# A two-layer decoder trunk on one core: the first layer's split weights kept in device memory, and the stick-breaking scans chained through a column of their own

## The chip, the core and the metric

The kernel runs on one core of one Trainium2 chip. The core has five engines with a queue of instructions each: TensorE (PE in the profile; its weight loads are listed apart as PEld), VectorE (DVE), ScalarE (ACT), GpSimd (POOL) and SyncE (SP), which here issues every DMA. The engines run side by side and wait for one another through semaphores. Data lies in device memory, in SBUF (128 partitions) and in PSUM, where matmuls accumulate.

The metric is the device time of one execution in microseconds, lower is better; each kernel is timed in several runs, and one further execution is recorded by the hardware profiler.

## The reference

The input is 2048 tokens of width 1024, with 16 learned meta tokens put in front: 2064 tokens. Two layers follow, each as h = h + post_norm(mixer(pre_norm(h))). The mixer of layer 0 has two branches from one input projection (22 blocks of 128 columns): sliding-window attention with sinks, and a convolution module. The mixer of layer 1 is stick-breaking attention, 16 heads of width 64.

```python
def swa_conv_mixer(h, pos, w_in, sinks, conv_w, conv_b, ln_g, ln_b, w_pw2, w_out):
    q, k, v, g_a, glu_in, g_b = _split(h @ w_in, AB_SPLITS)
    ...
    a = sliding_window_sink_attention(q, k, v, sinks).reshape(b, l, SWA_WIDTH) * jax.nn.silu(g_a)
    u = glu_in[..., :CONV_CHANNELS] * jax.nn.sigmoid(glu_in[..., CONV_CHANNELS:])
    c = jax.nn.silu(layer_norm(causal_depthwise_conv(u, conv_w, conv_b), ln_g, ln_b))
    c = (c @ w_pw2) * jax.nn.silu(g_b)
    return jnp.concatenate([a, c], axis=-1) @ w_out

def stick_breaking_attention(q, k, v):
    ...
        log_beta = jax.nn.log_sigmoid(z)
        log_1m = jnp.where(valid, jax.nn.log_sigmoid(-z), 0.0)
        after = lax.cumsum(log_1m, axis=3, reverse=True) - log_1m
        a = jnp.where(valid, jnp.exp(log_beta + after), 0.0)
        outs.append(jnp.einsum('bhqk,bkhd->bqhd', a.astype(v.dtype), vp[:, :kend]))
```

In words, for each query the weight of a key is sigmoid(z) times the product of sigmoid(-z) over all later valid keys. The convolution has 31 taps.

## The kernel before

**Split matmuls.** A float32 matmul is made of three in the faster format fp32r: each operand is split into a rounded half and the rest (`wh` and `wl` for weights, `hTh` and `hTl` for activations), and `mm3` (lines 126 to 130) adds high x high, high x low and low x high. A weight block is 128 x 8 x 128 floats, 512 KB. A projection of 512 tokens by one block is 24 matmuls of 512 columns.

**Layer 0.** The tokens go in four chunks (528, then three times 512). `stage1(c)` normalizes and transposes a chunk and runs the 22 projections; `stage2(c)` is the attention (`swa`) and the end of the convolution branch (`cbranch`) of the chunk. `stage1(c + 1)` is interleaved with `stage2(c)`. The weights stay in no buffer from one chunk to the next: `weights` (lines 112 to 121) is called by every projection, 22 times per chunk, and twice by each of the eight `pw` steps of `cbranch` (the two halves of `w_pw2`), 104 times in all. Each call loads the raw block into `raw` (line 118; two buffers, for `w_pw2` one that is shared with the tile `yl`), ScalarE casts it to `wh` (line 119), and GpSimd subtracts to get `wl` (line 120). `wh` and `wl` have two buffers each in the pool `pww`. The load has a priority 60 steps ahead of its place.

The 31 convolution taps are VectorE instructions (line 294), four blocks of channels per chunk; they are put into a list and recorded six at a time behind the projections. Gates, rotary products, the splits of activations and the score masks are VectorE's too; GpSimd has part of the rotary work (lines 339 to 343) and small normalization steps (lines 88 to 93). All results of stage 1 go to device memory (`q0d`, `k0d`, `v0d`, `gad`, `gbd`, `yd`) on SyncE's queue and come back in stage 2. After the last chunk comes the output projection of layer 0, interleaved with the first loads of layer 1.

**Layer 1.** The projections (`proj`, their splits in lines 109 and 110) of one pair of heads are interleaved with the attention (`attn`) of an earlier pair. `attn` takes two query blocks of 128 (`x`) and two heads (`h`) at a time and walks the keys in chunks of up to 512 from the last to the first. For each of the four (h, x) of a chunk: two matmuls give `z` (line 898); ScalarE makes `om` = sigmoid(-z/8) and `be` = sigmoid(z/8) (lines 902, 903); in the first chunk, which holds the diagonal, GpSimd masks both (line 906); VectorE scans the running product of `om` from right to left into `S` (line 910) and multiplies `be` by `S` shifted by one column (line 913). The weights are transposed (line 930), copied by ScalarE (line 936) and multiplied with the values (line 944).

The scan's start value lies in `S[:, n]`. For a first chunk GpSimd fills it with 1.0 (line 907); for the others it copies it from the tile `carry` (line 909), into which it copied the last product `S[:, 0]` of the chunk before (line 912). `om` and `S` have three buffers, `be` two for each (h, x). GpSimd also copies the weights of the meta tokens (line 915).

**The order.** The program is recorded step by step; a scheduler then orders each engine's queue by a simulated timeline and priorities. Every queue runs in order: an instruction that waits holds up all behind it. On SyncE a DMA also waits for the one eight places ahead that used the same semaphore.

Of the kernel before, what the change touches and what calls it, by code (L numbers as in the profile page):

```python
# [10 lines left out]
F32 = mybir.dt.float32  # L11
F32R = mybir.dt.float32r
I32 = mybir.dt.int32
AF = mybir.ActivationFunctionType
ALU = mybir.AluOpType
# [3 lines left out]
P = 128  # L19
D = 1024  # L20
KB = D // P
# [16 lines left out]
WP = 60  # L38
# [40 lines left out]
class Trunk:  # L79
# [29 lines left out]
        self.nc.gpsimd.tensor_scalar(hi, src, 1.0, 0.0, ALU.mult, ALU.add)  # L109
        self.nc.vector.tensor_tensor(lo, src, hi, ALU.subtract)  # L110

    def weights(self, pool, src, rpool, tag):
        nc = self.nc
        raw = rpool.tile([P, KB, P], F32, tag=tag, name="raw", bufs=2 if tag == "raw" else 1)
        wh = pool.tile([P, KB, P], F32R, tag="wh", name="wh")
        wl = pool.tile([P, KB, P], F32R, tag="wl", name="wl")
        with self.tc.high_priority(offset=WP):
            self.wdma = nc.sync.dma_start(raw, src).ins
        nc.scalar.copy(wh, raw)  # L119
        nc.gpsimd.tensor_tensor(wl, raw, wh, ALU.subtract)  # L120
        return wh, wl

    def mv(self, out, src):
# [54 lines left out]
    def layer0(self, after=None):  # L178
        tc, nc, a = self.tc, self.nc, self.a
        HALO = CW - 1  # L180
        qd = self.dram("q0d", [P, 2, 4, T], F32R)
        kd = self.dram("k0d", [2, 2, HD, T], F32R)
# [68 lines left out]
        def stage1(c):  # L251
# [23 lines left out]
            steps.append((0.0, start))  # L275

            def proj(m, evac):
                wh, wl = self.weights(pww, a["w_in0"][m], s1, "raw")
                turns = late[:]
                late.clear()  # L280
                for s0, sn in subs:
                    ps = self.bank(next(banks), "pj")
                    for k in range(KB):
                        self.mm3(ps[:, :sn], wh[:, k], wl[:, k], st["h"][:, k, s0 : s0 + sn], st["l"][:, k, s0 : s0 + sn], k == 0, k == KB - 1)
                    evac(ps[:, :sn], s0, sn)
                for f in turns:
                    f()
# [191 lines left out]
        def cbranch(ut):  # L479
            b0 = tok0(ut[0])  # L480
            N = sum(toks(t) for t in ut)
            S = {}

            def stats():
                yl = w2.tile([P, 4, 272], F32, tag="yl", name="yl", bufs=1)
                nc.sync.dma_start(yl[:, :, :N], yd[:, :, b0 : b0 + N].rearrange("r p t -> p r t"))
                mv = w2.tile([P, 3, 2], F32, tag="mv", name="mv")
                nc.vector.memset(mv, 1.0)
                S["yns"] = yns = []
                for i, t in enumerate(ut):  # L490
                    n, o = toks(t), tok0(t) - b0
                    pt = self.bank("pt", "pt_y")
                    for j in range(4):
                        nc.tensor.transpose(pt[:n, j * P : j * P + P], yl[:, j, o : o + n], self.ident)
                    st = w2.tile([P, 6], F32, tag="bst", name="bst")
                    nc.vector.bn_stats(st[:n], pt[:n])
                    nc.vector.bn_aggr(mv[:n, i], st[:n])
                    yn = w3.tile([P, 512], F32, tag="yn", name="yn")
                    nc.scalar.copy(yn[:n], pt[:n])
                    yns.append(yn)  # L500
                cr = w2.tile([P, 3], F32, tag="cr", name="cr")
                self.rsqrt(w2, cr, mv[:, :, 1], 1.0, LEPS, 3, nc.gpsimd)
                for i, t in enumerate(ut):
                    n = toks(t)
                    nc.vector.tensor_scalar(yns[i][:n], yns[i][:n], mv[:n, i, 0:1], cr[:n, i : i + 1], ALU.subtract, ALU.mult)

            def act():
                yns = S["yns"]
                S["ch"] = ch = w2.tile([P, 4, 272], F32R, tag="ch", name="ch", bufs=1)
                S["cl"] = cl = w2.tile([P, 4, 272], F32R, tag="cl", name="cl", bufs=1)  # L510
                for j in range(4):
                    pt = self.bank("pt", "pt_c")
                    for i, t in enumerate(ut):
                        n, o = toks(t), tok0(t) - b0
                        nc.tensor.transpose(pt[:, o : o + n], yns[i][:n, j * P : j * P + P], self.ident[:n, :n])
                    sg = w2.tile([P, 272], F32, tag="csg", name="csg")
                    tt = w2.tile([P, 272], F32, tag="ctt", name="ctt")
                    nc.scalar.activation(sg[:, :N], pt[:, :N], AF.Sigmoid, bias=cv[:, 2, j : j + 1], scale=cv[:, 1, j : j + 1])
                    nc.scalar.activation(tt[:, :N], pt[:, :N], AF.Identity, bias=cv[:, 2, j : j + 1], scale=cv[:, 1, j : j + 1])
                    nc.vector.tensor_tensor(tt[:, :N], tt[:, :N], sg[:, :N], ALU.mult)  # L520
                    nc.scalar.copy(ch[:, j, :N], tt[:, :N])
                    nc.vector.tensor_tensor(cl[:, j, :N], tt[:, :N], ch[:, j, :N], ALU.subtract)

            def pw():
                ch, cl = S["ch"], S["cl"]
                gb = w2.tile([P, 4, 272], F32, tag="gb", name="gb", bufs=1)
                nc.sync.dma_start(gb[:, :, :N], gbd[:, :, b0 : b0 + N].rearrange("r p t -> p r t"))
                for m in range(4):
                    if m % 2 == 0:
                        wh, wl = self.weights(pww, a["w_pw2"][m // 2], w2, "yl")  # L530
                    ps = self.bank("pj", "pw")
                    for k in range(4):
                        kk = 4 * (m % 2) + k
                        self.mm3(ps[:, :N], wh[:, kk], wl[:, kk], ch[:, k, :N], cl[:, k, :N], k == 0, k == 3)
                    tt = w2.tile([P, 272], F32, tag="ctt", name="mc")
                    nc.vector.tensor_tensor(tt[:, :N], ps[:, :N], gb[:, m, :N], ALU.mult)
                    nc.sync.dma_start(md[4 + m, :, b0 : b0 + N], tt[:, :N])

            return stats, act, pw
# [269 lines left out]
    def layer1(self):  # L809
# [12 lines left out]
        def attn(p, hf):  # L822
# [53 lines left out]
            def pair_steps(m):  # L876
                es = edges(2 * m + 2)
                steps.append((0.0, lambda: qload(m)))
                carry = c1.tile([P, 4], F32, tag="carry", name="carry", bufs=2) if len(es) > 1 else None
                qc0 = (2 * m % 4) * P  # L880

                def chunk(ei):
# [7 lines left out]
                    for h in range(2):  # L890
                        for x in range(2):
                            n = nbs[x] * P + mo
                            if n == 0:
                                continue
                            ci = carry[:, 2 * h + x : 2 * h + x + 1] if carry is not None else None
                            z = self.bank("pz", "z")
                            for i in range(2):
                                nc.tensor.matmul(z[:, :n], S["q"][2 * h + i][:, x * P : x * P + P], S["k"][h][:, k0 : k0 + n], start=(i == 0), stop=(i == 1))  # L898
                            om = w3.tile([P, 512], F32, tag="om", name="om")
                            be = w2.tile([P, 512], F32, tag=f"be{h}{x}", name="be")  # L900
                            P_ = w3.tile([P, 513], F32, tag="S", name="S")
                            nc.scalar.activation(om[:, :n], z[:, :n], AF.Sigmoid, scale=-0.125)  # L902
                            nc.scalar.activation(be[:, :n], z[:, :n], AF.Sigmoid, scale=0.125)  # L903
                            if first:
                                for tt, fill in ((om, 1.0), (be, 0.0)):
                                    nc.gpsimd.affine_select(tt[:, n - P : n], tt[:, n - P : n], [[-1, P]], ALU.is_gt, fill, base=0, channel_multiplier=1)  # L906
                                nc.gpsimd.memset(P_[:, n : n + 1], 1.0)
                            else:
                                nc.gpsimd.tensor_scalar(P_[:, n : n + 1], ci, 1.0, 0.0, ALU.mult, ALU.add)  # L909
                            nc.vector.tensor_tensor_scan(P_[:, :n][:, ::-1], om[:, :n][:, ::-1], om[:, :n][:, ::-1], P_[:, n : n + 1], ALU.mult, ALU.bypass)  # L910
                            if not last:
                                nc.gpsimd.tensor_scalar(ci, P_[:, 0:1], 1.0, 0.0, ALU.mult, ALU.add)  # L912
                            nc.vector.tensor_tensor(be[:, :n], be[:, :n], P_[:, 1 : n + 1], ALU.mult)  # L913
                            if last:
                                nc.gpsimd.tensor_scalar(S["am"][:, 2 * m % 4 + x, h], be[:, :NM], 1.0, 0.0, ALU.mult, ALU.add)
                            bes[h, x] = be
# [203 lines left out]
```

## Time and profile before

| what | value |
|---|---|
| median of 3 runs | 2995.03 us (2994.13 to 2998.02) |
| the profiled execution | 2996.4 us, of which the recorded span is 2994.7 us |
| busy: PE / PEld | 2761.3 us (92%) / 2211.2 us (74%), 16110 instructions each |
| busy: DVE | 2358.1 us (79%), 3656 instructions |
| busy: ACT | 1518.2 us (51%), 3607 instructions |
| busy: POOL | 1483.4 us (50%), 2580 instructions |
| DMA | 395.77 MB, mean 132 GB/s |
| the chain that ended last | PE 60%, DVE 21%, issue 6%, POOL 5%, ACT 4%, DMA 3% |

"Busy" is the time in which an engine had an instruction running. The chain is followed back from the last instruction: at each step to what released it, or to the instruction before it on its engine. Rows of instruction groups read: line, engine, operation, output<-inputs, shapes, count | busy time, mean duration in ns | idle time of the engine just before them, and what ended it. Rows of a timeline read: start in us, duration in us, engine, line, operation, tiles, count, and in brackets the idle time before and what ended it. Durations of overlapping matmuls include their drain; the distance of their starts is their rate.

### The profile page before, as it was taken

To read this page: it belongs to the slowest core of one execution; us is meant where nothing else is said; L and a number is where in the kernel's file an instruction comes from. 1 tells how busy PE (TensorE), PEld (TensorE's weight loads), DVE (VectorE), ACT (ScalarE), POOL (GpSimd) and SP (SyncE) were. 2 spreads that over 40 slices of the span, in tenths; PEclk is the share of its full clock that TensorE was granted. 3 is DMA by queue.
4 is the path that set the end of the run, shared out by engine and by line. 5 is a ranking of instruction groups with operands and counts; after the bars stand their busy time and mean duration, and the time that the engine had idled before them with its cause. 6 is when DMAs were issued, how large, how long until landed. Compare 5 with 4: busy or idle time off the path is not lost.

```text
span 2994.7 us, 49703 instructions
## 1 busy us (share of the span) xinstructions
PE 2761.3 (92%) x16110; PEld 2211.2 (74%) x16110; DVE 2358.1 (79%) x3656; ACT 1518.2 (51%) x3607; POOL 1483.4 (50%) x2580
## 2 busy tenths in 40 slices
PE   7788897887899999999999899999999999989998
PEld 6776676676668789888888677777777767766776
DVE  7989989989977683566667888788787888887874
ACT  4224343433455532455544566676676666755551
POOL 4645546455421122354445766565565566665430
PEclk9889898998999999999999999999999999999999
DMA  4445555455476566344445554234242332344322
GB/s 160 141 133 148 154 166 142 148 163 147 137 203 199 175 219 183 116 131 133 132 134 171 168 137 119 86 86 114 68 111 64 100 100 72 92 121 127 106 96 88
DMA packets 285556, 395.77 MB, mean 132 GB/s; under 512 B 44593, under 2 KB 198593, under 8 KB 282225
## 3 DMA queue, kind: packets, MB, share of 16 engines
q1 hardware_dynamic: 285296, 392.59, 44.4%
q8 instruction: 129, 2.11, 0.3%
q14 instruction: 131, 1.07, 0.1%
HBM read 270.21 MB, written 116.97 MB: 129 GB/s over the span
## 4 chain that ended last, share of the span: by engine, by line
PE 60%; DVE 21%; issue 6%; POOL 5%; ACT 4%; DMA 3%; SPq 1%; DVEq 0%; POOLq 0%; ACTq 0%
DVE y L294 11%; PE pj L128 8%; PE pj L129 8%; PE pj L130 8%; PE z L898 7%; PE av L944 7%; PE pt L930 7%; PE po L128 4%; PE po L130 4%; PE po L129 3%; DVE S L910 2%; ACT om L902 1%; DMA raw<-in_w_in 1%; DVE p L446 1%; ACT be L903 1%
## 5 line engine op out<-in xcount | busy, mean ns | idle before, releaser
L910 DVE TENSOR_TENSOR_SCAN S<-om,S 128x384 f32<-128x384 f32 (+5 forms) x768 | 744.2, 988 | 150.3 <-POOL om L906 67.7
L294 DVE SCALAR_TENSOR_TENSOR y<-u,cw,y 128x512 f32<-128x512 f32 (+1 forms) x480 | 515.4, 1079 | 7.3
L902 ACT ACTIVATE om<-z 128x384 f32<-128x384 f32 (+5 forms) x768 | 379.3, 512 | 209.5 <-PE z L898 135.2
L128 PE MATMUL pj<-th,wh 128*128 128x512 f32 (+2 forms) x1280 | 460.7, 360 | 8.0 <-POOL wh L109 4.5
L913 DVE TENSOR_TENSOR be<-be,S 128x384 f32<-128x384 f32 (+5 forms) x768 | 403.0, 549 | 72.7 <-ACT be L903 33.8
L130 PE MATMUL pj<-th,wl 128*128 128x512 f32 (+2 forms) x1280 | 452.4, 353 | 0.3 <-DVE wl L110 0.3
L129 PE MATMUL pj<-tl,wh 128*128 128x512 f32 (+2 forms) x1280 | 451.2, 352 | 0.0
L936 ACT COPY aT<-pt 128x512 f32<-128x512 f32 (+2 forms) x672 | 334.8, 505 | 201.2 <-PE pt L930 157.0
L898 PE MATMUL z<-kst,qt 128*128 128x384 f32 (+6 forms) x1536 | 396.4, 358 | 28.1 <-ACT be L903 26.9
L903 ACT ACTIVATE be<-z 128x384 f32<-128x384 f32 (+5 forms) x768 | 375.9, 506 | 76.5 <-PE pt L930 75.8
L930 PE MATMUL pt<-ident,be 128*128 128x128 f32 x2176 | 363.3, 281 | 24.3 <-ACT aT L936 9.7
L120 POOL TENSOR_TENSOR wl<-raw,wh 128x1024 fp32r<-128x1024 f32 x104 | 273.4, 2631 | 177.1 <-ACT wh L119 176.9
L912 POOL TENSOR_SCALAR carry<-S 128x1 f32<-128x1 f32 x512 | 265.8, 521 | 184.8 <-DVE S L910 160.3
L130 PE MATMUL pj<-hTh,wl 128*128 128x512 f32 (+2 forms) x880 | 321.7, 368 | 25.3 <-POOL wl L120 25.3
L930 PEld LDWEIGHTS pt<-ident,be 128*128 128x128 f32 x2176 | 252.7, 141 | 120.5 <-ACT aT L936 35.1
L128 PE MATMUL pj<-hTh,wh 128*128 128x512 f32 (+2 forms) x880 | 325.8, 371 | 12.3 <-DVE gt L366 6.4
L909 POOL TENSOR_SCALAR S<-carry 128x1 f32<-128x1 f32 x512 | 263.6, 517 | 136.6 <-DVE be L913 116.5
L129 PE MATMUL pj<-hTl,wh 128*128 128x512 f32 (+2 forms) x880 | 322.6, 367 | 1.3 <-DVE hTl L176 1.3
L898 PEld LDWEIGHTS z<-kst,qt 128*128 128x128 f32 x1536 | 249.0, 191 | 72.6 <-ACT be L903 51.9
L944 PE MATMUL av<-aT,vt 128*64 128x256 f32 (+1 forms) x2304 | 282.1, 381 | 4.6 <-DVE og L962 4.6
L128 PEld LDWEIGHTS pj<-th,wh 128*128 128x128 f32 x1280 | 241.8, 189 | 35.0 <-POOL wh L109 4.9
L130 PEld LDWEIGHTS pj<-th,wl 128*128 128x128 f32 x1280 | 240.9, 188 | 30.0 <-DVE wl L110 0.6
(177 smaller groups left out, 4817.4 us busy)
## 6 DMA issues: line engine op xcount, KB each, us to landing
raw<-in_w_in SPq DMA_DIRECT2D x164, 512.0 KB, 3.7
qt<-qhd SPq DMA_DIRECT2D x256, 64.0 KB, 2.6
qt<-qld SPq DMA_DIRECT2D x256, 64.0 KB, 2.4
kst<-khd SPq DMA_DIRECT2D x16, 516.0 KB, 7.8
kst<-kld SPq DMA_DIRECT2D x16, 516.0 KB, 10.0
qT<-q0d SPq DMA_DIRECT2D x32, 256.0 KB, 3.6
raw<-in_w_pw SPq DMA_DIRECT2D x16, 512.0 KB, 3.9
rawo<-in_w_out SPq DMA_DIRECT2D x16, 512.0 KB, 4.5
```

The lines of the kernel that those rows point to most:

```text
L128: mm(out, sh, mh, start=first, stop=False)
L129: mm(out, sh, ml, start=False, stop=False)
L130: mm(out, sl, mh, start=False, stop=last)
L294: return lambda: nc.vector.scalar_tensor_tensor(y[:, :TC], u[:, w : w + TC], cw[:, j, w : w + 1], y[:, :TC], ALU.mult, ALU.add)
L898: nc.tensor.matmul(z[:, :n], S["q"][2 * h + i][:, x * P : x * P + P], S["k"][h][:, k0 : k0 + n], start=(i == 0), stop=(i == 1))
L902: nc.scalar.activation(om[:, :n], z[:, :n], AF.Sigmoid, scale=-0.125)
L903: nc.scalar.activation(be[:, :n], z[:, :n], AF.Sigmoid, scale=0.125)
L910: nc.vector.tensor_tensor_scan(P_[:, :n][:, ::-1], om[:, :n][:, ::-1], om[:, :n][:, ::-1], P_[:, n : n + 1], ALU.mult, ALU.bypass)
L913: nc.vector.tensor_tensor(be[:, :n], be[:, :n], P_[:, 1 : n + 1], ALU.mult)
L930: nc.tensor.transpose(pt[:, o : o + P], bes[h, x][:, mo + b * P : mo + b * P + P], self.ident)
L936: cps.append(nc.scalar.copy(aT[:, lo:hi], pt[:, lo:hi]))
L944: mi = nc.tensor.matmul(av[h * HD : h * HD + HD, qc0 + x0 : qc0 + 256], S["v"][:, b0 + b, h * HD : h * HD + HD], at, start=not S["started" ...
```

## The change

There are two parts. In layer 0, the first call of `weights` for a block (22 blocks of `w_in0`, all in chunk 0, and two halves of `w_pw2`) makes the split as before and stores `wh` and `wl` to a tile in device memory, `wk0` to `wk21` and `wp0`, `wp1`. Each later call loads both halves from there straight into `wh` and `wl`, two DMAs of 512 KB, with the priority that the raw load had; there is no `raw`, no cast and no subtraction in it.

In layer 1, `om` and `be` get one more column. `om[:, n]` is filled with 1.0 on GpSimd, and so is the column ahead of `be` (`bl[:, 0]`). The scan runs over n + 1 columns and starts from 1.0, or from `lead`, the column `bl[:, 0]` of the chunk before; the product runs over n + 1 columns too, so that `bl[:, 0]` becomes 1.0 times the last product of the scan. `carry` and the two copies by GpSimd are gone.

```diff
-    def weights(self, pool, src, rpool, tag):
+    def weights(self, pool, src, rpool, tag, kept):
         nc = self.nc
+        if kept in self.drams:
+            wh = pool.tile([P, KB, P], F32R, tag="wh", name="wh")
+            wl = pool.tile([P, KB, P], F32R, tag="wl", name="wl")
+            with self.tc.high_priority(offset=WP):
+                for i, w in enumerate((wh, wl)):
+                    self.mv(w, self.drams[kept][:, i])
+            return wh, wl
+        kd = self.dram(kept, [P, 2, KB, P], F32R)
         raw = rpool.tile([P, KB, P], F32, tag=tag, name="raw", bufs=2 if tag == "raw" else 1)
...
         nc.scalar.copy(wh, raw)
         nc.gpsimd.tensor_tensor(wl, raw, wh, ALU.subtract)
+        for i, w in enumerate((wh, wl)):
+            self.mv(kd[:, i], w)
         return wh, wl
...
-                wh, wl = self.weights(pww, a["w_in0"][m], s1, "raw")
+                wh, wl = self.weights(pww, a["w_in0"][m], s1, "raw", f"wk{m}")
...
-                        wh, wl = self.weights(pww, a["w_pw2"][m // 2], w2, "yl")
+                        wh, wl = self.weights(pww, a["w_pw2"][m // 2], w2, "yl", f"wp{m // 2}")
...
-                carry = c1.tile([P, 4], F32, tag="carry", name="carry", bufs=2) if len(es) > 1 else None
+                lead = {}
...
-                            om = w3.tile([P, 512], F32, tag="om", name="om")
-                            be = w2.tile([P, 512], F32, tag=f"be{h}{x}", name="be")
+                            om = w3.tile([P, 513], F32, tag="om", name="om")
+                            bl = w2.tile([P, 513], F32, tag=f"be{h}{x}", name="be")
+                            be = bl[:, 1:]
+                            nc.gpsimd.memset(om[:, n : n + 1], 1.0)
+                            nc.gpsimd.memset(bl[:, 0:1], 1.0)
...
-                                nc.gpsimd.memset(P_[:, n : n + 1], 1.0)
-                            else:
-                                nc.gpsimd.tensor_scalar(P_[:, n : n + 1], ci, 1.0, 0.0, ALU.mult, ALU.add)
-                            nc.vector.tensor_tensor_scan(P_[:, :n][:, ::-1], om[:, :n][:, ::-1], om[:, :n][:, ::-1], P_[:, n : n + 1], ALU.mult, ALU.bypass)
-                            if not last:
-                                nc.gpsimd.tensor_scalar(ci, P_[:, 0:1], 1.0, 0.0, ALU.mult, ALU.add)
-                            nc.vector.tensor_tensor(be[:, :n], be[:, :n], P_[:, 1 : n + 1], ALU.mult)
+                            init = lead[h, x] if (h, x) in lead else 1.0
+                            nc.vector.tensor_tensor_scan(P_[:, : n + 1][:, ::-1], om[:, : n + 1][:, ::-1], om[:, : n + 1][:, ::-1], init, ALU.mult, ALU.bypass)
+                            nc.vector.tensor_tensor(bl[:, : n + 1], bl[:, : n + 1], P_[:, : n + 1], ALU.mult)
+                            lead[h, x] = bl[:, 0:1]
```

How the queues change is seen in the order of the two programs. The first place is SyncE's queue where chunk 1 begins. Before, the loads of the raw blocks (`raw`, numbered by buffer) stand between stores of gates (`gbd`) and taps (`yd`) and the first loads of stage 2, and wait for GpSimd, which frees `raw`:

```order
L369 DMA gbd_83<-gt_1822 128x528 [waits DMAHW4_49,DVE_49]
L118 DMA raw_2113<-in_w_in0 128x1024 [waits DMAHW1_49,Pool_49]
L369 DMA gbd_83<-gt_1892 128x528 [waits DMAHW6_49,DVE_49]
L118 DMA raw_2156<-in_w_in0 128x1024 [waits DMAHW7_49,DMAHW3_49,Pool_49]
L527 DMA gb_3700<-gbd_83 128x4x272 [waits DMAHW4_49,DMAHW2_49,DMAHW6_49,DMAHW0_49,PE_49]
L298 DMA yd_84<-y_1514 128x528 [waits DVE_49]
L124 DMA qT_2223<-q0d_79 128x4x128 [waits PE_49]
```

Of the change, the same place, with the last stores of chunk 0's halves (`wk21`) and the first loads of kept ones (`wk14`, `wk10`):

```order
L134 DMA wk21_1956<-wh_1958 128x1024 [waits DMAHW4_49,Activation_49]
L134 DMA wk21_1956<-wl_1959 128x1024 [waits DMAHW5_49,Pool_49]
L134 DMA wh_2031<-wk14_249 128x1024 [waits DMAHW6_49,DMAHW0_49,PE_49]
L134 DMA wl_2032<-wk14_249 128x1024 [waits DMAHW7_49,DMAHW2_49,PE_49]
L379 DMA gbd_83<-gt_1882 128x528 [waits DVE_49]
L134 DMA wh_2106<-wk10_313 128x1024 [waits DMAHW4_49,DMAHW1_49,PE_49]
L134 DMA wl_2107<-wk10_313 128x1024 [waits DMAHW5_49,PE_49]
L379 DMA gbd_83<-gt_1955 128x528 [waits DMAHW3_49,DVE_49]
L308 DMA yd_84<-y_1562 128x528 [waits DVE_49]
```

The loads now wait for TensorE, which frees `wh` and `wl`, and gate stores that wait for VectorE still stand between them.

The second place is GpSimd's queue in layer 1, at a pair of query blocks with two chunks of keys. Before, fills and copies of `S` alternate with the masks of `om` and `be`; each copy into `carry` waits for a scan on VectorE:

```order
L906 AFFINE_SELECT om_18469<-om_18469 128x128 [waits Activation_49]
L912 TENSOR_SCALAR carry_18064<-S_18455 128x1 [waits DVE_49]
L906 AFFINE_SELECT be_18470<-be_18470 128x128 [waits PE_49,Activation_49]
L907 MEMSET S_18503 128x1 [waits DVE_49,Pool_49]
L906 AFFINE_SELECT om_18485<-om_18485 128x128 [waits Activation_49]
L912 TENSOR_SCALAR carry_18064<-S_18471 128x1 [waits DVE_49]
L906 AFFINE_SELECT be_18486<-be_18486 128x128 [waits PE_49,Activation_49]
L909 TENSOR_SCALAR S_18551<-carry_18064 128x1 [waits DVE_49,Pool_49]
```

Of the change, at the same pair:

```order
L918 AFFINE_SELECT om_18461<-om_18461 128x128 [waits Activation_49]
L911 MEMSET om_18493 128x1 [waits DVE_49]
L918 AFFINE_SELECT be_18462<-be_18462 128x128 [waits Activation_49]
L912 MEMSET be_18568 128x1 [waits PE_49]
L912 MEMSET be_18581 128x1 [waits PE_49]
L918 AFFINE_SELECT om_18477<-om_18477 128x128 [waits Activation_49]
L911 MEMSET om_18541 128x1 [waits DVE_49]
L918 AFFINE_SELECT be_18478<-be_18478 128x128 [waits Activation_49]
```

The copies that waited for scans are gone. Fills for tiles of the next chunk stand between the masks; a fill of `om` waits for an earlier scan that used the buffer, a fill of `be` for TensorE's transposes of the buffer's last contents.

More of the change, by code (lines that the diff above doesn't have):

```diff
@@ L894, in chunk @@
                                 continue
-                            ci = carry[:, 2 * h + x : 2 * h + x + 1] if carry is not None else None
                             z = self.bank("pz", "z")
```

## The prediction

> **What bounds the kernel now.** I read the page first: the forty slices, 75 us each, show where an engine waits.
>
> ```profile
> span 2994.7 us, 49703 instructions
> ...
> PE   7788897887899999999999899999999999989998
> DVE  7989989989977683566667888788787888887874
> PEclk9889898998999999999999999999999999999999
> DMA  4445555455476566344445554234242332344322
> ```
> TensorE (PE) is busy at 9 tenths from slice 12 (the 900 us mark) to nearly the end, and mostly at 7 or 8 before that, where its granted clock is below full speed too. VectorE (DVE) is the reverse: mostly 9 until slice 11, then 5 to 8. So the first 850 us, the first layer's projections, belong to VectorE and the rest to TensorE. The windows view, cut about where one chunk of tokens follows another in layer 0:
>
> ```profile
> core 0: us, PE busy (x) PEld busy (x) DVE busy (x) ACT busy (x) POOL busy (x), PEclk, DMA share, GB/s
> 0.00:210.00 210.00, 161.78 (x1163) 155.23 (x1163) 186.96 (x215) 63.86 (x110) 114.27 (x99) 0.94 0.44 138
> 210.00:430.00 220.00, 188.63 (x893) 148.46 (x894) 203.78 (x359) 91.99 (x207) 110.09 (x108) 0.93 0.56 160
> 430.00:650.00 220.00, 183.24 (x874) 145.22 (x874) 203.23 (x317) 86.06 (x171) 117.09 (x93) 0.90 0.52 155
> 650.00:850.00 200.00, 173.43 (x833) 136.42 (x833) 183.75 (x297) 78.66 (x164) 94.77 (x66) 0.93 0.51 145
> 850.00:1125.00 275.00, 264.76 (x1380) 214.78 (x1379) 206.49 (x517) 146.95 (x295) 49.17 (x64) 0.98 0.67 199
> 1575.00:2775.00 1200.00, 1139.50 (x6850) 858.28 (x6849) 979.52 (x1308) 759.59 (x1879) 750.48 (x1544) 0.99 0.37 108
> ```
> The columns are the window, its length, the busy time of PE, PEld, DVE, ACT and POOL, the clock, the share of the 16 DMA engines and the GB/s. From 210 to 850 us, three chunks of tokens in 640 us, VectorE is busy 203.78 + 203.23 + 183.75 = 590.8 us, 92%. The chain that ended last says the same for the first of the three:
>
> ```profile
> by line: DVE y L294 35.5%; issue 10.9%; PE pj L128 4.6%; PE pj L129 4.3%; DVE p L446 4.2%; DVE p L430 3.7%; PE pj L130 3.7%; POOL wl L120 2.6%; DMA kT<-k0d 2.1%; POOL rs_t L92 2.0%; DVE qr L338 1.8%; DVE qr L340 1.7%; DMA raw<-in_w_pw 1.7%;
> ```
> The convolution taps of line 294 are 35.5% of it. They are slow for a reason that two rows of the timelines show, VectorE first, then GpSimd (POOL):
>
> ```profile
> 438.12 2.79 DVE L294 SCALAR_TENSOR_TENSOR y<-u,cw,y 128x512 f32<-128x512 f32 x1
> ```
> ```profile
> 437.96 2.40 POOL L120 TENSOR_TENSOR wl<-raw,wh 128x1024 fp32r<-128x1024 f32 x1
> ```
> The tap that started while GpSimd formed a `wl` took 2.79 us. Most taps take far less:
>
> ```profile
> L294 DVE SCALAR_TENSOR_TENSOR y<-u,cw,y x480: 699/752/3007, 38.4 to 836.5; 128x512 f32<-128x512 f32 x120, 128x528 f32<-128x528 f32 x40
> ```
> The median is 752 ns. So VectorE is the bound of those 640 us in part because it stands still behind GpSimd's `wl` instructions.
>
> **The change, part one: split weights kept.** 104 calls make a `wl` now; after the change 24 do, and 80 read both halves back. The windows view of line 120 alone:
>
> ```profile
> 0.00:210.00 210.00, 67.74 (x25) 0.94 0.44 138
> 210.00:850.00 640.00, 191.31 (x73) 0.92 0.53 154
> 850.00:1125.00 275.00, 14.33 (x6) 0.98 0.67 199
> ```
> 22 of the first 25 and 2 of the 73 stay (chunk 0, and the first use of each half of `w_pw2`), so 3, 71 and 6 go. What one costs VectorE is bounded by rows of the middle window:
>
> ```profile
> L294 DVE SCALAR_TENSOR_TENSOR y<-u,cw,y 128x512 f32<-128x512 f32 (+1 forms) x365 | 383.7, 1056 | 5.0
> ```
> ```profile
> L120 POOL TENSOR_TENSOR wl<-raw,wh 128x1024 fp32r<-128x1024 f32 x73 | 191.3, 2623 | 136.0 <-ACT wh L119 135.7
> L339 POOL TENSOR_TENSOR qs<-qs,stab 128x512 f32<-128x512 f32 x15 | 25.6, 1705 | 20.1 <-DMA qs<-qr 18.3 <-PE pj L130 1.0 <-PE s L429 0.8
> L343 POOL TENSOR_TENSOR qr<-qr,qs 128x512 fp32r<-128x512 f32 x15 | 24.4, 1628 | 1.1
> ```
> The 365 taps lost 365 x (1056 - 752) ns = 111 us. Three GpSimd lines of two inputs run beside them, 191.3 + 25.6 + 24.4 = 241.3 us; `wl` has 79% of that, and 71 of its 73 go, so the taps get 86 us back, 1.2 us for each `wl`. That is the low end, since the taps are 383.7 of VectorE's 590.8 us and the other lines lose too. The high end is the pair of rows above: 2.79 - 0.75 = 2.04 us. I take 1.6 us, the middle: 71 x 1.6 = 114 us, and VectorE's work becomes 591 - 114 = 477 us.
>
> TensorE is then late next. Its busy time of the three windows, put at full clock, is 188.63 x 0.93 + 183.24 x 0.90 + 173.43 x 0.93 = 502 us. The clock sank because TensorE waited for VectorE:
>
> ```profile
> 457.09 0.82 PE L429 MATMUL s<-kT,qT 128*128 128x272 f32 x2 [5.43 <-DVE mx L430]
> ...
> 459.56 0.63 PE L128 MATMUL pj<-hTh,wh 128*128 128x512 f32 x1
> 459.99 0.60 PE L129 MATMUL pj<-hTl,wh 128*128 128x512 f32 x1
> ...
> 460.65 0.40 PE L128 MATMUL pj<-hTh,wh 128*128 128x512 f32 x1
> 460.89 0.40 PE L129 MATMUL pj<-hTl,wh 128*128 128x512 f32 x1
> ```
> After 5.43 us without work the matmuls start 0.43 us apart, and some 3 us later 0.24 us. With shorter waits the clock should come up, so I count 502 us. The Trainium skill, page "TensorE: Matmul & The Clock Gate", Part 1, says that the clock halves after an idle window of about 3.4 us and comes back after a busy one as long; by that rule waits under that length cost no clock and the 502 us hold, and the trace agrees in this one place (0.43 us apart, then 0.24).
>
> With 502 and 477 us of work two engines are nearly level, and neither reaches what one alone does: VectorE got to 92% as the clear bound, TensorE to 264.76 of 275 us (96%) behind 850 us with VectorE at 75%, and TensorE is at 545 of 640 us (85%) now. I take 89%: 502 / 0.89 = 564 us, a gain of **76 us**; the ends are 502 / 0.96 = 523 (117) and 502 / 0.85 = 590 (50).
>
> What it adds is transfers. A load of 512 KB on SyncE's (SP) queue now:
>
> ```profile
> L118 SPq DMA_DIRECT2D raw<-in_w_in x88: 327/372/743, 2.7 to 811.4; - x88
> ...
> DMA to landing us min/median/max: 3.1/3.9/9.7
> ```
> Issuing takes 0.37 us, landing 3.9 us from there. Now one load of 512 KB runs ahead into `raw`; afterwards two load straight into `wh` and `wl`, and each waits until TensorE has finished the weight before last. Two issues, 3.9 us, and 1.8 us for the second's bytes (512 KB at 154 GB/s over a DMA share of 0.53, from the middle window) make 6.4 us. TensorE uses a weight for 24 x 0.24 = 5.8 us, and its other work is (502 - 66 x 5.8) / 66 = 1.8 us per weight, together 7.6. With two buffers the loop can turn every (6.4 + 7.6) / 2 = 7.0 us, and 564 / 66 = 8.5 us are wanted: hidden, with 1.5 us to spare. It becomes the bound when a load takes over 2 x 8.5 - 7.6 = 9.4 us, waiting in SyncE's queue included. The saved ACT casts (1.05 us) and GpSimd time lie beside other work and count nothing more.
>
> Chunk 0 gets the 44 stores. They are 44 x 0.37 = 16 us on SyncE and 44 x 1.8 = 79 us of all DMA engines, in 210 us with a DMA share of 0.44: about 0.8, not full. Its 22 `wl` stay, so VectorE (187 of 210 us) stays the bound. In the queue a store that waits for GpSimd stands ahead of the next `raw` load, which had to wait for that same instruction before. I take **+4 us**, between 0 and +20 (the issues bare). Behind 850 us TensorE is the bound and 6 `wl` go: **-3 us** (0 to -12, 6 x 2.04).
>
> **Part two: no GpSimd copies in layer 1.** From 1575 to 2775 us the chain is TensorE's:
>
> ```profile
> by line: PE z L898 13.2%; PE av L944 12.0%; PE pt L930 11.6%; PE pj L128 10.0%; PE pj L129 9.9%; PE pj L130 9.8%; issue 7.1%; DVE S L910 4.9%; ACT om L902 2.4%; DMA raw<-in_w_in 1.8%; DVE be L913 1.8%; ACT be L903 1.5%; POOL om L906 1.3%; P
> ```
> The groups concerned, and the single-column fill of line 907:
>
> ```profile
> L910 DVE TENSOR_TENSOR_SCAN S<-om,S 128x384 f32<-128x384 f32 (+5 forms) x768 | 744.2, 988 | 150.3 <-POOL om L906 67.7
> ...
> L913 DVE TENSOR_TENSOR be<-be,S 128x384 f32<-128x384 f32 (+5 forms) x768 | 403.0, 549 | 72.7 <-ACT be L903 33.8
> ...
> L912 POOL TENSOR_SCALAR carry<-S 128x1 f32<-128x1 f32 x512 | 265.8, 521 | 184.8 <-DVE S L910 160.3
> ...
> L909 POOL TENSOR_SCALAR S<-carry 128x1 f32<-128x1 f32 x512 | 263.6, 517 | 136.6 <-DVE be L913 116.5
> ```
> ```profile
> L907 POOL MEMSET S<- x256: 88/94/108, 1124.6 to 2848.7; 128x1 f32 x128
> ```
> 1024 copies of some 519 ns go (529 us of GpSimd), and 1280 more fills at 94 ns come (120 us); the fills run between 88 and 108 ns, so nothing on VectorE stretches them. Each scan and product gets one column: 768 x (988 + 549) / 384 ns = 3 us of VectorE. VectorE's 150.3 us of idle time before scans ended 67.7 us with GpSimd's mask of `om`, which stands in the queue behind such copies. But TensorE is busy 1139.5 of these 1200 us and GpSimd's mask has 1.3% of the chain, 16 us. The most to gain is TensorE's whole rest, 60 us. What can be lost: a fill of `be` now waits for TensorE's transposes, with masks, `am` copies and the `wh` of the next projection behind it on GpSimd, and a scan's start now needs the product of the chunk before, hence its second sigmoid. If one in ten of the 768 tiles is held by 0.5 us that is 38 us on VectorE, of which a third, some 13 us, may reach TensorE. I take **-10 us**, between -60 and +13, nearest to the 16 us of the chain.
>
> **Sum.** The profiled execution took 2996.4 us (its span 2994.7), 1.4 us above the median of the runs, 2995.03. 2996.4 + 4 - 76 - 3 - 10 = 2911; in terms of the median **2910 us**.
>
> **Rivals.** (1) *More comes free*: each `wl` blocks VectorE for its whole length, and the loads never show. Then TensorE gets to 96%: -117, layer 1 -25, behind 850 us -3: 2851. For it: the tap of 2.79 us lasts past the whole 2.40 us. Against: the taps' mean gives 1.2 us. The Trainium skill, page "SBUF — State Buffer", section "SBUF: two separate sides", calls the ports that VectorE and GpSimd share an exclusive lock held for a whole instruction; by that, 71 x 2.6 us (the row of `wl`) come free, 186 us; the single tap agrees, the 1.2 us do not reach it.
> (2) *Only part arrives*: loads stand in SyncE's queue behind a store that waits for VectorE.
>
> ```profile
> SPq L369 <- DVE gt L366: 71.0, 15, 9.0
> ```
> At 71.0 / 15 = 4.7 us more, a load takes 11.1 us, a weight 9.35, the window 617 us: -23, in all 2964. If the clock stays at its 0.92, 545 / 0.89 = 612 us come to the same.
> (3) *The taps are slow for another reason*, and the removed work lay beside other work anyway: layer 1's -10 against +4 in chunk 0, 2990. The overlap of start times speaks against it.
> (4) *Slower*: each load into `wh`/`wl` is late. The prefetch loses two stages (`raw` had two buffers of its own). From 2 x 640 / 66 - 7.6 = 11.8 us per load on, the window is longer than now. With 7 us in the queue (the longest such wait is 9.0) it is 13.4, a weight takes 10.5, the window 693 us: +53 +4 -13, 3040. Against it: the waits are VectorE's, and VectorE is what gets relieved.
>
> **How the numbers follow.** Forecast 0.56 (its own range 2880 to 2940, from the 50 to 94 us, 94 being 92% for TensorE, and layer 1 at either side), rival 1 0.14, rival 2 0.18, rival 3 0.04, rival 4 0.08. 0.2% (6 us) is about what a measurement of this kernel can tell from no change. Faster by more: 0.56 + 0.14 + 0.18 = 0.88; within 0.04; slower 0.08. The range 2850 to 2970 takes in rivals 1 and 2.
>
> **What would show it.** Right: the mean of line 294's taps falls to about 850 ns from chunk 1 on, its median stays; windows of about 188 us per chunk at a clock near 1.00, TensorE ahead of VectorE; 24 `wl` instructions; chunk 0 within 20 us of 198. Wrong: TensorE waiting for the DMA of `wh` or `wl` in rows of its own (rival 2 or 4), taps still at 1056 ns (rival 3), scans waiting for fills (part two). If layer 1's stage from 1575 to 2775 us changes by over 25 us either way, part two is mis-sized.

## The result and the profile after

The changed kernel takes **2944.83 us** (median of 4 runs, 2937.36 to 2949.58) against 2994.58 us (4 runs, 2991.28 to 2998.02): ratio 0.9831, 95% interval 0.9807 to 0.9856, a gain of some 50 us. The prediction was 2910 us, range 2850 to 2970. The sign is right and the time lies in the range, but outside the forecast's own 2880 to 2940. The profiled execution took 2946.3 us, its span 2944.6 us. (Of the runs below, one of the kernel with the fill, at 2937 us, is in a slower state of the chip, with a granted clock of 0.89 in place of 0.99, and its ratio leaves that run out.) Its page, the slices of 74 us each:

```profile
span 2944.6 us, 49666 instructions
...
PE   7788989979999999999999999999999999998997
...
DVE  7988878877777763566667888878887887887864
...
PEclk9999999999999999999999999999999999999999
DMA  7777877787785765444445553323232332244322
```

In slices 4 to 11 (about 220 to 810 us) TensorE is now mostly at 9, VectorE at 7 or 8; in the first 11 slices the DMA engines went from 4 or 5 to 7 or 8. The windows view of both kernels, cut at the first matmul of chunk 1, the last of chunk 3, and the first and the last scores of layer 1, before and then after (columns as in the prediction):

```profile
0.00:198.60 198.60, 155.71 (x1133) 150.50 (x1134) 175.74 (x204) 59.70 (x105) 109.29 (x97) 0.94 0.45 142
198.60:833.60 635.00, 536.28 (x2533) 424.10 (x2532) 592.02 (x958) 255.82 (x537) 324.54 (x266) 0.92 0.52 150
833.60:1150.00 316.40, 304.86 (x1644) 248.49 (x1643) 221.44 (x548) 156.76 (x316) 53.80 (x69) 0.98 0.68 202
1150.00:2902.00 1752.00, 1686.65 (x10443) 1325.98 (x10442) 1330.04 (x1867) 1026.09 (x2613) 989.40 (x2142) 0.99 0.39 114
```

```profile
0.00:199.20 199.20, 156.84 (x1139) 151.68 (x1139) 175.45 (x214) 59.51 (x105) 111.92 (x96) 0.94 0.75 257
199.20:792.10 592.90, 530.17 (x2530) 415.84 (x2531) 472.04 (x950) 192.38 (x468) 123.08 (x194) 0.95 0.77 229
792.10:1104.00 311.90, 302.01 (x1638) 245.59 (x1637) 214.50 (x546) 147.51 (x307) 33.25 (x70) 0.99 0.72 216
1104.00:2852.00 1748.00, 1683.98 (x10443) 1324.48 (x10442) 1329.41 (x1867) 1026.97 (x2612) 585.56 (x2390) 0.99 0.39 115
```

| stage | before, us | after, us | change | predicted |
|---|---|---|---|---|
| chunk 0 | 198.6 | 199.2 | +0.6 | +4 |
| chunks 1 to 3 | 635.0 | 592.9 | -42.1 | -76 |
| up to layer 1's first scores | 316.4 | 311.9 | -4.5 | -3 |
| from there to the end of the span | 1844.7 | 1840.6 | -4.1 | -10 |

Of the 35 us by which the time missed the forecast, 34 lie in the row of chunks 1 to 3. VectorE's busy time there fell from 592.02 to 472.04 us, as forecast (591 to 477), yet the stage didn't follow. What TensorE waited for in chunks 1 to 3 (the waits view: total us, times, longest) says why. Before:

```profile
PE s L429 <- DVE mx L430: 47.6, 19, 6.0
PE pw L128 <- DVE mc L536: 18.4, 4, 8.4
...
PE pj L130 <- POOL wl L120: 6.0, 4, 2.8
```

After:

```profile
PE pj L138 <- DMA wh<-wk: 22.1, 11, 4.1
PE pj L140 <- DMA wl<-wk: 14.6, 9, 6.6
PE s L439 <- DVE mx L440: 12.2, 6, 3.2
PE pw L138 <- DVE mc L546: 3.6, 2, 2.1
```

The waits for VectorE's `mx` and `mc` fell from 66.0 to 15.8 us, and 36.7 us of waits for the kept weights took their place: the sign of rivals 2 and 4.

### The profile page after: what moved, and what is told of

Its sections match the earlier page's. It is cut to its first block, busy times and chain, and to the rows that moved or that the text cites. A ratio compares the mean times of both kernels' runs of the same rounds, so it can differ in the third digit from the quotient of the medians.

```text
span 2944.6 us, 49666 instructions
## 1 busy us (share of the span) xinstructions
PE 2750.7 (93%) x16110; PEld 2199.4 (75%) x16110; DVE 2230.2 (76%) x3656; ACT 1446.3 (49%) x3529; POOL 860.3 (29%) x2756
## 4 chain that ended last, share of the span: by engine, by line
PE 67%; DVE 10%; DMA 9%; issue 5%; POOL 4%; ACT 3%; SPq 2%; DVEq 0%; ACTq 0%; POOLq 0%
PE pj L140 10%; PE pj L138 10%; PE pj L139 10%; PE z L907 7%; PE av L953 7%; PE pt L939 6%; PE po L138 4%; PE po L140 4%; PE po L139 4%; DVE S L920 2%; DVE y L304 2%; DMA wl<-wk 2%; DMA raw<-in_w_in 2%; DVE be L921 1%; DMA qs<-qr 1%
## 5 line engine op out<-in xcount | busy, mean ns | idle before, releaser
L920 DVE TENSOR_TENSOR_SCAN S<-om,be 128x401 f32<-128x401 f32 (+3 forms) x512 | 535.7, 1067 | 72.7 <-ACT om L914 51.7
L921 DVE TENSOR_TENSOR be<-be,S 128x385 f32<-128x385 f32 (+5 forms) x768 | 413.3, 563 | 75.5 <-POOL be L912 21.8
L304 DVE SCALAR_TENSOR_TENSOR y<-u,cw,y 128x512 f32<-128x512 f32 (+1 forms) x480 | 424.7, 886 | 9.4
L140 PE MATMUL pj<-hTh,wl 128*128 128x512 f32 (+2 forms) x880 | 322.4, 369 | 34.0 <-POOL wl L128 19.3
L911 POOL MEMSET om<- 128x1 f32 x768 | 74.7, 99 | 770.2 <-DVE S L920 755.3
L139 PEld LDWEIGHTS pj<-tl,wh 128*128 128x128 f32 x1280 | 241.5, 189 | 25.2 <-issue 0.4
L920 DVE TENSOR_TENSOR_SCAN S<-om 128x257 f32<-128x257 f32 (+4 forms) x256 | 204.7, 811 | 63.2 <-POOL om L918 50.5
```

What stands on the lines that cost most here:

```text
L139: mm(out, sh, ml, start=False, stop=False)
L140: mm(out, sl, mh, start=False, stop=last)
L304: return lambda: nc.vector.scalar_tensor_tensor(y[:, :TC], u[:, w : w + TC], cw[:, j, w : w + 1], y[:, :TC], ALU.mult, ALU.add)
L920: nc.vector.tensor_tensor_scan(P_[:, : n + 1][:, ::-1], om[:, : n + 1][:, ::-1], om[:, : n + 1][:, ::-1], init, ALU.mult, ALU.bypass)
L921: nc.vector.tensor_tensor(bl[:, : n + 1], bl[:, : n + 1], P_[:, : n + 1], ALU.mult)
```

## The experiments

Each time is a median; ratios are to the kernel before, run on the same chip.

**1. What does GpSimd's subtraction cost VectorE?** First it is taken away and a fill with zeros put there (in the kernel before, line 120; the low halves of the weights are then left out), then put back into the changed kernel, where nothing needs it:

```diff
-        nc.gpsimd.tensor_tensor(wl, raw, wh, ALU.subtract)
+        nc.gpsimd.memset(wl.bitcast(F32), 0.0)
```

> The kernel before, with each of the 104 subtractions on GpSimd replaced by a fill of wl with zeros, so the low halves of the weights are left out; raw loads and casts stay, and no byte of transfer is added. It asks what GpSimd's subtraction costs VectorE when nothing is put in its place. Theory (the taps are slow because GpSimd reads two tiles in SBUF at the same time): the mean of the taps falls from 1079 to 900 ns or less, chunk 0 gets about 20 us shorter and chunks 1 to 3 take 545 to 570 us in place of 635, in all 2885 to 2915. Rival, any long GpSimd instruction on SBUF slows VectorE: the mean stays above 1000 ns and the time above 2975.

```diff
                     self.mv(w, self.drams[kept][:, i])
+            if tag == "raw":
+                raw = rpool.tile([P, KB, P], F32, tag=tag, name="raw", bufs=2)
+                nc.gpsimd.tensor_tensor(raw, wh, wl, ALU.subtract)
             return wh, wl
```

> The changed kernel, in which GpSimd subtracts wl from wh into the free buffers of raw once for each kept weight of w_in0: 66 two-input instructions of the size of the removed ones are put back, off the path of the weights; the result is not used. Theory (each costs VectorE 1.2 to 2.0 us, and VectorE then is the bound beside late loads): VectorE's busy time in chunks 1 to 3 goes from 472 us back to 550 to 600, the mean of the taps from 886 to 1000 or more, and the time to 2990 to 3020. Rival (the removed instruction cost through GpSimd being late, not through VectorE): the taps stay below 920 ns, and the time stays within 10 us of 2945.

The fill: 2852.1 us (4 runs, three of them from 2849 to 2852.4 and one at 2937), ratio 0.952 (0.9501 to 0.9539), a larger gain than the theory had foreseen. The subtraction put back: 2996.2 us (10 runs, 2992.25 to 3001.0), ratio 1.0005 (0.9996 to 1.0014); the whole gain of the change is gone, as the theory expected. The windows of chunk 0 and of chunks 1 to 3 with the fill, and its groups of the taps and of the fill in chunks 1 to 3 (count, busy us, mean ns):

```profile
0.00:167.40 167.40, 145.06 (x1134) 141.80 (x1135) 136.29 (x209) 59.83 (x105) 68.42 (x97) 0.99 0.55 173
167.40:694.00 526.60, 504.12 (x2513) 401.16 (x2513) 468.84 (x951) 259.64 (x538) 195.84 (x266) 0.98 0.61 180
```

```profile
L294 DVE SCALAR_TENSOR_TENSOR y<-u,cw,y 128x512 f32<-128x512 f32 (+1 forms) x366 | 291.4, 802 | 5.4
```

```profile
L120 POOL MEMSET wl<- 128x1024 f32 x74 | 71.1, 960 | 155.1 <-PE pj L130 118.6 <-PE pw L130 11.4 <-PE pt_m L453 9.2
```

With the subtraction back in the changed kernel, the window of chunks 1 to 3 and the same groups:

```profile
199.40:839.00 639.60, 544.40 (x2531) 426.97 (x2532) 571.43 (x945) 195.37 (x470) 299.59 (x260) 0.92 0.71 213
```

```profile
L307 DVE SCALAR_TENSOR_TENSOR y<-u,cw,y 128x512 f32<-128x512 f32 (+1 forms) x362 | 373.2, 1031 | 6.8
```

```profile
L122 POOL TENSOR_TENSOR raw<-wh,wl 128x1024 f32<-128x1024 f32 x66 | 167.0, 2530 | 186.2 <-DMA wl<-wk 186.0
```

With the fill the taps take 802 ns on average, with the subtraction back 1031; chunks 1 to 3 take 526.6 and 639.6 us. In the second run the buffers are held until GpSimd has read them too, but later loads don't explain its loss. TensorE's waits in chunks 1 to 3 there:

```profile
PE s L442 <- DVE mx L443: 42.1, 15, 7.9
PE pj L141 <- DMA wh<-wk: 18.3, 9, 5.1
PE pw L141 <- DVE mc L549: 9.0, 3, 7.3
...
PE pj L143 <- DMA wl<-wk: 6.8, 7, 3.0
PE s L442 <- DMA wh<-wk: 3.3, 1, 3.3
```

It waits 28.4 us for kept weights, less than the 36.7 of the change, and 51.1 us for VectorE's `mx` and `mc` in place of 15.8. The mechanism holds from both sides, and it is not any GpSimd instruction that does it: 74 fills of 960 ns leave the taps alone. Counted over all of VectorE's instructions in layer 0 (what each takes above the 5th percentile of its line and shape, put down to the GpSimd instruction that it overlaps longest):

```
                                  instructions   lost by VectorE   each
before, subtractions                  104           175.5 us      1.69 us
after, subtractions                    24            40.2 us      1.68 us
put back, line 122                     66           107.5 us      1.63 us
fills in their place                  104            10.0 us      0.10 us
```

The Trainium skill, page "SBUF — State Buffer", section "Who interferes with whom", says that a VectorE instruction with two inputs in SBUF contends with a GpSimd instruction that reads SBUF and not with one that only writes it; the fill agrees (0.10 us lost for 0.96 us of fill, 1.63 for 2.53 us of the subtraction put back). The run with the fill also spares the wait of `wl` for `raw`, so its 108 us in chunks 1 to 3 (635.0 - 526.6) are not all VectorE's; of TensorE's own waits, those for `wl` fell only from 6.0 to 3.4 us there. It keeps the 512 KB of `raw` per weight, which have buffers of their own.

**2. Why does TensorE wait for kept weights?** Three causes are possible: the bytes, the place in SyncE's queue, or too few buffers. The first run gives a third pair of buffers (the two of `raw`, idle from chunk 1 on), with the same bytes on the same queue:

```diff
-            wh = pool.tile([P, KB, P], F32R, tag="wh", name="wh")
-            wl = pool.tile([P, KB, P], F32R, tag="wl", name="wl")
+            self.turn = getattr(self, "turn", 0) + (tag == "raw")
+            if tag == "raw" and self.turn % 3 == 0:
+                wh, wl = (rpool.tile([P, KB, P], F32R, tag="raw", name=n, bufs=2) for n in ("wh", "wl"))
+            else:
+                wh = pool.tile([P, KB, P], F32R, tag="wh", name="wh")
+                wl = pool.tile([P, KB, P], F32R, tag="wl", name="wl")
```

> The changed kernel, in which every third kept weight of w_in0 goes into the two buffers of raw, which are free from chunk 1 on: three pairs of buffers in place of two, the same bytes, the same queue. Theory: the loads are late because they are issued late, each after TensorE has freed a buffer and whatever then stands ahead of it in SyncE's queue, so that TensorE waits 41 us for wh and wl in chunks 1 to 3. A third pair gives one more weight (9 us) of notice: half to three quarters of the 41 us go, the clock follows from 0.95 towards 1.00, and the time is 2910 to 2925. Rival, the bytes: at a DMA share of 0.78 the transfers themselves are the bound, then nothing comes of it, 2940 to 2948.

The second leaves two pairs and takes the loads off SyncE's queue:

```diff
-                    self.mv(w, self.drams[kept][:, i])
+                    nc.scalar.dma_start(w.bitcast(F32), self.drams[kept][:, i].bitcast(F32))
```

> The changed kernel with the loads of kept halves issued by ScalarE, two pairs of buffers as in the change. If the order in SyncE's queue (loads behind stores and other loads, and qs, kT, ga behind loads that wait for TensorE) is what costs, TensorE's 41 us of waits fall to about 10 and the time is 2910 to 2920. If two pairs of buffers are too few whatever the queue, it stays within 5 us of 2945. A third outcome: a load that waits for TensorE on ScalarE's queue holds up the copies out of PSUM that stand behind it, TensorE waits for ScalarE in their place, and it takes 2950 to 2990.

Three pairs: **2901.0 us** (5 runs, 2895.49 to 2902.39), ratio 0.9681 (0.9668 to 0.9695). Loads on ScalarE: 2933.5 us (4 runs, 2931.61 to 2935.58), ratio 0.9789 (0.9776 to 0.9802). The windows of chunks 1 to 3 and TensorE's waits for kept weights, three pairs first:

```profile
201.80:745.10 543.30, 511.73 (x2518) 407.29 (x2515) 463.30 (x937) 194.78 (x469) 135.96 (x194) 0.97 0.82 250
```

```profile
PE pj L142 <- DMA wh<-wk: 4.3, 4, 2.3
PE pj L144 <- DMA wl<-wk: 3.0, 4, 1.2
```

Loads on ScalarE:

```profile
199.00:774.90 575.90, 525.95 (x2529) 412.75 (x2530) 469.82 (x949) 191.03 (x469) 127.63 (x194) 0.95 0.79 236
```

```profile
PE pj L140 <- DMA wl<-wk: 8.1, 8, 2.4
...
PE pj L138 <- DMA wh<-wk: 5.1, 4, 2.4
```

The bytes are not the bound: with three pairs more pass per second (250 GB/s against 229, DMA share 0.82 against 0.77), and TensorE's waits for weights fall from 36.7 to 7.3 us. The place in SyncE's queue is a cost of its own: off that queue the same loads into the same two pairs leave 13.2 us of waits, and the stage is 17 us shorter. It gave less than the theory's 2910 to 2920, so the queue is only a part. The time with three pairs, 2901.0, is below the theory's 2910 to 2925. The third pair is worth 50 us of the stage (592.9 to 543.3), more than the 36.7 us of waits (the expectations say 41; these rows of the view give 36.7): TensorE's busy time fell too, from 530.17 to 511.73 us, at a clock of 0.97 in place of 0.95.

How late loads come about is seen in SyncE's queue of the changed kernel (start, duration to issue, DMA):

```profile
648.93 0.50 SPq L134 DMA_DIRECT2D wh<-wk  x1
649.53 0.38 SPq L367 DMA_DIRECT2D v0d<-vt  x1
652.17 0.50 SPq L330 DMA_DIRECT2D q0d<-qs  x1
653.86 0.50 SPq L330 DMA_DIRECT2D q0d<-qr  x1
654.41 0.59 SPq L330 DMA_DIRECT2D q0d<-qs  x1
655.05 0.59 SPq L330 DMA_DIRECT2D q0d<-qr  x1
655.74 0.55 SPq L367 DMA_DIRECT2D v0d<-vt  x1
656.38 0.39 SPq L134 DMA_DIRECT2D wl<-wk  x1
```

and TensorE at that time:

```profile
662.57 0.80 PE L140 MATMUL pj<-hTh,wl 128*128 128x512 f32 x1 [6.64 <-DMA wl<-wk]
```

`wl` is issued 7.45 us after its own `wh`, behind stores of rotary results and of `v` that wait for GpSimd and ScalarE; it lands 6.1 us later, and TensorE stands still for 6.64 us. For each of the 71 kept weights loaded in these windows, the time from the end of the last matmul that read the buffers' old contents to the landing of `wl`, worked out from the traces (a load may be issued up to 0.2 us ahead of that modelled end):

```
us                       median  mean  90th percentile  over 9.4   issued over 1 us late
after                     6.6    7.9        13.1        19 of 71         23
loads on ScalarE          6.2    6.8         9.9         8 of 71         10
```

9.4 us is the prediction's bound. Of the 19 loads above it 16 were issued over 1 us late; the transfers alone, from the issue of `wh` to the landing of `wl`, have a median of 6.3 us. In the other direction the loads hold up SyncE's queue too, since two of three are issued as soon as TensorE frees the buffer:

```profile
SPq L134 <- PE pj L140: 131.6, 34, 10.5
...
SPq L379 <- DVE gt L376: 24.3, 21, 4.1
```

For 131.6 us the queue stood at such a load, with whatever came behind it. Two variants of the three pairs ask what is left, loads on ScalarE's queue and loads 120 steps ahead:

```diff
+                    nc.scalar.dma_start(w.bitcast(F32), self.drams[kept][:, i].bitcast(F32))
```

> Three pairs of buffers, as in the run before it, with the loads of kept halves issued by ScalarE. If the queue's order is a cost of its own, apart from the number of buffers, TensorE's last waits for wh and wl go (7 us) and SyncE's other transfers come earlier: 2885 to 2895. If the third pair has already hidden what the queue did, 2898 to 2906. If loads that wait for TensorE hold up ScalarE's copies out of PSUM, 2910 or more.

```diff
-            with self.tc.high_priority(offset=WP):
+            with self.tc.high_priority(offset=120):
```

> Three pairs of buffers, and the loads of kept halves 120 steps ahead of their place in place of 60. If the loads that are still issued late are so because of their place in the queue, 2890 to 2898. If earlier places only make SyncE's queue wait for TensorE longer, with qs, kT and ga behind it, 2902 to 2920. If 60 steps were enough, 2898 to 2903.

The first takes 2908.4 us (4 runs, ratio 0.972, 0.9701 to 0.9739), between its second and third outcome: slower than on SyncE's queue, if anything. The second takes 2899.8 us (4 runs, ratio 0.9688, 0.9673 to 0.9703), the same as three pairs alone. So with the third pair neither the queue nor an earlier place is worth more. Three pairs on SyncE beat both kernels by a clear margin.

The Trainium skill, page "DMA: Bandwidth & Descriptors", section "Issuing engines are not separate DMA queues", says that issuing from several engines saves only the sequencer's time to issue. Here, with two pairs, it saved 17 us of a stage, and loads issued over 1 us late went from 23 to 10 of 71; with three pairs it saved nothing. In SyncE's rows above, the seven issues from `wh` up to `wl` take 3.61 of the 7.45 us, and the rest are waits of the queue for other engines. So the order of waits has a part in what was saved, beside the time to issue; how the 17 us divide between the two, no run here shows.

**3. Each part alone.** Layer 1 put back in the changed kernel, and part two alone in the kernel before; each is the diff shown in the change, with the other part left out.

> The changed kernel with layer 1 put back as it was before: only the split weights are kept. If the two parts add up as the milestones of the two profiles say (chunks 1 to 3 shorter by 42 us, the time up to the first scores of layer 1 by 46 us, the rest by 4 us), this takes 2994.6 - 46 = 2949 us, 4 us more than the changed kernel. If part two is worth the 10 us that the prediction gave it, 2955. If part two costs time (new waits of scans for fills), it is at or below the changed kernel, 2940 to 2945.

> The kernel before with part two alone. By the milestones 2994.6 - 4 = 2991 us; by the prediction's term 2985; if the fills that wait for transposes hold the masks up, 2995 to 3000. The stage up to the first scores of layer 1 is the same as before within 2 us.

Part one alone: 2946.5 us (4 runs, 2941.09 to 2950.57), ratio 0.9831 (0.9818 to 0.9845). Part two alone: 2991.8 us (11 runs), ratio 0.9987 (0.9978 to 0.9996), so 3 to 4 us (1 to 7). On top of part one it is too small to be seen (2944.8 against 2946.5). What TensorE waited for in layer 1, from the first scores to the last, before:

```profile
PE z L898 <- ACT be L903: 26.9, 53, 2.6
...
PE pj L128 <- POOL wh L109: 4.5, 2, 2.4
```

With part two alone:

```profile
PE z L897 <- ACT be L905: 29.2, 53, 2.4
...
PE pj L128 <- POOL wh L109: 2.6, 1, 2.6
```

GpSimd's busy time there fell from 989.40 to 585.56 us in the full change, and TensorE, the bound, hardly ever waited for GpSimd: 4.5 us in 1752. Its longest row, the scores that wait for ScalarE to read the PSUM bank, is not touched. The wait that the change adds, GpSimd's fill of `be` behind TensorE's transposes, is there and stays off TensorE's path:

```profile
POOL be L902 <- PE pt L929: 108.0, 139, 4.7
```

## Why the prediction was right, and where its sizes were off

**VectorE's relief: right.** 1.6 us for each `wl` between bounds of 1.2 and 2.04; the traces give 1.63 to 1.69. VectorE's busy time in chunks 1 to 3 was forecast at 477 us and is 472. The taps of all chunks fell from 1079 to 886 ns (850 forecast from chunk 1 on; there they are below it):

```profile
L304 DVE SCALAR_TENSOR_TENSOR y<-u,cw,y 128x512 f32<-128x512 f32 (+1 forms) x367 | 298.6, 814 | 7.0
```

**TensorE is late next: right.** Its 502 us at full clock are 530.17 x 0.95 = 504 after.

**The term that failed: "hidden, with 1.5 us to spare".** The prediction took a load as a constant of 6.4 us and set it against 9.4 us. The median is 6.6 us, so the constant was good; but the loads spread to 13 us and more, and one in four passed the bound. TensorE waited 36.7 us for them, where the prediction had put nothing. With a third pair of buffers, on the same queue and with the same bytes, 7.3 us are left, so two pairs were too small a reserve for loads that spread so far.

**The clock did not come up as counted.** "With shorter waits the clock should come up, so I count 502 us": it stayed at 0.95. In chunks 1 to 3 of the changed kernel the trace's clock record has 15 stretches of 3.4 or 6.8 us at half clock, 64.9 us together. Seven begin in or behind a wait for a kept weight and six in or behind a wait for VectorE, and at 12 of the 15 no single wait was over 3.2 us. One of them, first the wait, then the clock in a window before it and in one behind it (third number from the end):

```profile
292.88 0.52 PE L439 MATMUL s<-kT,qT 128*128 128x272 f32 x2 [2.80 <-DVE mx L440]
```

```profile
286.60:290.10 3.50, 3.48 (x26) 2.94 (x24) 3.50 (x5) 1.34 (x3) 2.09 (x3) 1.00 0.50 139
293.40:296.80 3.40, 3.37 (x12) 1.62 (x10) 3.14 (x7) 0.00 (x0) 3.15 (x5) 0.51 0.38 89
```

So the rule by which the 502 us would hold, that waits under about 3.4 us cost no clock, is not borne out here; which of the shorter waits cost clock and which don't, the runs do not show.

Together these make TensorE fill 504 / 592.9 = 85% of the stage in place of 89%. That is 593 us against the 564 forecast (and the 590 of its low end), 29 of the 34 us; the rest is the cut (the prediction's windows gave 640 us to what is 635 here). With the third pair TensorE gets below the forecast, 543.3 us.

**The 89% was two things at once.** The prediction took its 85 and 96% from shares of busy time, at clocks of 0.92 and 0.98, put 89% between them, and divided work at full clock by it. In busy time TensorE did reach 530.17 / 592.9 = 89%, but by luck, since the reason given, two engines nearly level, is not what held it down. With the fill the two are as level, 504.12 x 0.98 = 494 us of TensorE's work at full clock and 468.84 of VectorE's, and TensorE is busy 504.12 of the 526.6 us, 96% (at full clock 94%). So the relief alone was worth up to 108 us, near the 117 of rival 1, whose condition (loads that never show) the third pair comes near and the change doesn't; the loads into two pairs took up to 66 of it back (592.9 - 526.6). The prediction stated 76 for the relief and nothing for the loads. Of the 17 us between the three pairs and the fill, the runs don't tell how much is transfers, and how much the fill that needs no `raw`.

**Rival 2 named the right place, and its price was too high.** Loads do stand in SyncE's queue behind stores that wait for another engine (GpSimd's and ScalarE's results as well as VectorE's gates, whose waits fell to 24.3 us). It put 4.7 us on every load; in fact one load in three was over 1 us late. It gave 2964, and the time, 2944.8, lies between it and the forecast. Rival 3 fell with the fill, rival 4's point of 11.8 us per load was passed by some 8 of the 71 loads.

**Chunk 0** was forecast at +4 and came to +0.6: the DMA engines went to a share of 0.75 (about 0.8 forecast) and the stores hide behind VectorE.

**Part two** was mis-sized, -10 for the 3 to 4 us measured. The step that failed is to price it by the chain's 16 us for GpSimd's masks: the waits view of TensorE itself gave 4.5 us to GpSimd, and that was readable before.

## What to carry to other kernels

When a compute step is replaced by a load into the same buffers, count how many stages ahead the data now runs, and hold the spread of the load, its wait in an in-order queue included, against the slack, not its median. Here a GpSimd subtraction of two tiles in SBUF cost a busy VectorE about two thirds of its own length (1.63 us of 2.53); look there before counting GpSimd's work as free. And read the prize of a change from the waits of the bounding engine, by releaser, not from the idle time of the engine that is relieved.

## What was not expected of the hardware

How far the subtractions reach: 104 of them cost VectorE 175.5 us by the overlap count, and with none of them chunks 0 to 3 were 139.6 us shorter (833.6 to 694.0), 31 of these in chunk 0 (198.6 to 167.4), where the change keeps 22 and gains nothing. Not all of the 31 us came through VectorE: in chunk 0 TensorE's own waits for `wl` fell from 19.3 to 5.0 us with the fill. And a DMA share of 0.82 over 543 us did not stretch the loads enough to be the bound: from issue to the landing of both halves the median is 7.0 us there, against 6.3 us at 0.77.
